# Attention output of a sliding-window layer: two PSUM halves copied out by ScalarE for both heads and added by GpSimd, in place of one ScalarE copy and two VectorE adds

## The chip, the core and the metric

The kernel runs on one core of a Trainium2 chip. A core has five engines, each with its own instruction stream that it works through in order: TensorE (PE in the profile, with PEld for its weight loads), VectorE (DVE), ScalarE (ACT), GpSimd (POOL) and SyncE (SP, which here only starts transfers). They share a large memory, SBUF, of 128 partitions. Matrix products land in PSUM, which has eight banks of 128 partitions by 512 float32 columns; GpSimd does not read PSUM in this kernel. The metric is the time in microseconds of one execution on the device, the median of several runs.

## What is computed

One layer of the reference, cut to what matters here (2048 tokens, width 2048, 32 query heads of 64, 4 key/value heads, blocks of 128 queries that see themselves and the 128 tokens before):

```python
q, k, v, gate = split(rms_norm(x) @ w_in)
q, k = rms_norm(q) * q_gain, rms_norm(k) * k_gain
s = einsum('bqhgd,bkhd->bhgqk', qj, kb) * scale + bias      # 128 queries against 256 keys
s = where(valid, s, -inf)
m = maximum(max(s), sink)
p = exp(s - m)
p = p / (sum(p) + exp(sink - m))
o = einsum('bhgqk,bkhd->bqhgd', p, vb)
return x + (o * silu(gate)) @ w_out
```

## The kernel before

The queries, keys and values are made by matrix products of 128 by 512 (`gemm`, lines 148, 151 and 154). To keep precision each float32 operand is split into a high part and a low remainder, and three products are added: high by high, high by low, low by high. One step of the plan `steps` makes 128 columns of the projection for 1024 tokens: 96 such products into two banks. There are two halves of the tokens (`c`), and in each two groups of one key step, one value step and eight query steps. While a step's products run, the attention of queries made earlier is put beside them (`beside`, which calls `unit`). After that come the gate's and the output's products, in a scheme with 7 instead of 8 quarter products; they fill the second half of the time, and the change does not touch them.

One call of `unit` handles two heads and two blocks of 128 queries; there are 128 calls. In order:

- `s` (two PSUM banks, one buffer): eight products of queries by keys, line 329. VectorE masks (line 337) and writes the biased scores into `lg` (line 342, four instructions), after which the two banks are free for the next unit.
- VectorE takes the row maximum, ScalarE four exponentials (line 355), VectorE the sum and its reciprocal, GpSimd the normalising product (line 360).
- `pt` (one bank, one buffer): four transposes on TensorE, line 364. ScalarE copies them as the high part `ph` (line 366), VectorE makes the remainder `pl` (line 368). Both have one buffer.
- GpSimd splits each by a triangle into the part of the earlier and of the current block: `php`, `plp` (line 372), `ph`, `pl` (line 374, in place), one buffer each.
- `o` (one bank, one buffer): up to eight products of values by probabilities, line 383. The values' tile `vv` holds the high parts in its first 64 columns and the remainders in the other 64, so partitions 0 to 63 of `o` hold the high half's result and partitions 64 to 127 the low half's. They have to be added. The two heads lie side by side in `o`'s columns; they are to end up below each other in `og`, one head in partitions 0 to 63 and the other in 64 to 127.
- Lines 385 to 390 do that, and are what the change edits.

```python
bot = at.tile([DH, 4, P], F32, tag="bot", name="bot", bufs=1)
nc.scalar.copy(out=bot, in_=o[DH:P])
og = at.tile([P, 2, P], F32, tag="og", name="og", bufs=1)
for h in range(2):
    nc.vector.tensor_tensor(out=og[h * DH:(h + 1) * DH], in0=o[0:DH, h::2, :], in1=bot[:, h::2, :], op=ALU.add)
```

The order of instructions on each engine is not the order of the code. The program is built with `schedule_with_timeline_sim=True`: a scheduler goes over all of it with its own estimates of durations, follows what each buffer and each operand permits, and writes out one fixed order for every engine. An edit in `unit` can thus move any instruction of the attention's stretch, on every engine. At run time an engine takes its instructions in that fixed order, and waits by semaphores.

Of the kernel before, what the change touches and what calls it, by code (L numbers as in the profile page):

```python
# [9 lines left out]
F32 = mybir.dt.float32  # L10
# [3 lines left out]
ALU = mybir.AluOpType  # L14
AX = mybir.AxisListType

P = 128
# [7 lines left out]
DH = 64  # L25
# [6 lines left out]
def swa_layer_kernel(ctx: ExitStack, tc: tile.TileContext, xT: bass.AP, x: bass.AP, w_in: bass.AP,  # L32
# [13 lines left out]
    nc = tc.nc  # L46
# [8 lines left out]
    at = attention.enter_context(tc.tile_pool(name="at", bufs=2))  # L55
# [263 lines left out]
    def unit(cb, j, qq, rq, kk, vv, bt):  # L319

        i0 = j % 4
        hs = slice(2 * cb, 2 * cb + 2)
# [30 lines left out]
        for b in range(2):  # L353
            for h in range(2):
# [6 lines left out]
                                op=ALU.mult)  # L361
# [16 lines left out]
        o = ps_o.tile([P, 4, P], F32, tag="o", name="o")  # L378
        for b in range(2):
            terms = [] if first and b == 0 else [(vv[:, i0 + b, :], p) for p in prev]  # L380
            terms += [(vv[:, i0 + b + 1, :], p) for p in cur]
            for i, (v, p) in enumerate(terms):
                nc.tensor.matmul(o[:, 2 * b:2 * b + 2, :], v, p[:, 2 * b:2 * b + 2, :],  # L383
                                 start=(i == 0), stop=(i == len(terms) - 1))
        bot = at.tile([DH, 4, P], F32, tag="bot", name="bot", bufs=1)
        nc.scalar.copy(out=bot, in_=o[DH:P])
        og = at.tile([P, 2, P], F32, tag="og", name="og", bufs=1)
        for h in range(2):
            nc.vector.tensor_tensor(out=og[h * DH:(h + 1) * DH], in0=o[0:DH, h::2, :], in1=bot[:, h::2, :], op=ALU.add)
        nc.sync.dma_start(out=o_sp[cb][:, j * P:(j + 2) * P], in_=og.rearrange("p b q -> p (b q)"))  # L390


# [29 lines left out]
    def beside(n):  # L422

        for cb, j in units.get(n, []):
            c, half = j // NB, j % NB // 4
            if (cb, c) not in bias:
                bias[cb, c] = load_bias(cb)
            if (cb // 4, c, half) not in kv:
                kv[cb // 4, c, half] = load_kv(cb // 4, c, half)
            qs, rq = queries[cb, c]  # L430
            unit(cb, j, qs[half], rq, *kv[cb // 4, c, half], bias[cb, c])
# [257 lines left out]
    for m, (p, i) in enumerate(tiles):  # L689
        kind, name = flat[p]  # L690
# [85 lines left out]
```

## Time and profile before

| what | value |
|---|---|
| median of 3 runs | 2465.68 us (2463.45 to 2465.91) |
| profiled execution, its own time | 2466.36 us |
| its span, first to last instruction | 2464.6 us |
| TensorE busy | 2431.2 us (99%) |
| VectorE, ScalarE, GpSimd busy | 1648.4, 971.6, 1092.3 us |
| stretch with attention | about 125 to 1303 us of the span |

The span is the time between the first and the last instruction in the trace; 1.8 us of the execution lie around it. Busy time of TensorE is a union of modelled intervals: products overlap, so a product of 512 columns shows 0.39 us and is followed by the next after 0.23. Idle time that an engine shows before an instruction is put down to whatever ended the wait.

### The profile page before, as it was taken

The page shows a single profiled execution, that of the slowest core. Times are in us where ns is not written, and L with a number is a line of the kernel's source. Part 1 is how long each engine was busy: PE and PEld are TensorE (multiplying, and loading weights), DVE is VectorE, ACT ScalarE, POOL GpSimd, SP SyncE. Part 2 cuts the span into 40 slices and gives each one's busy share as a digit, 9 for nine tenths or more (in the row PEclk, how much of TensorE's full clock was granted, in tenths as well). Part 3 has the DMA queues.
Part 4 walks back from the last instruction along what each step waited for, and adds up shares of the span by engine and source line. Part 5 has one row for each costly group of instructions (what it writes and reads, how often), then busy time and mean ns, then how long its engine had stood idle before and what let it go on. Part 6 is the DMA issues. An engine that isn't in the chain of part 4 may idle for free.

```text
span 2464.6 us, 35291 instructions
## 1 busy us (share of the span) xinstructions
PE 2431.2 (99%) x11858; PEld 2044.4 (83%) x11858; DVE 1648.4 (67%) x3206; ACT 971.6 (39%) x2387; POOL 1092.3 (44%) x1041
## 2 busy tenths in 40 slices
PE   8999999999999999999999999999999999999999
PEld 7888888887788888888887888888888888888887
DVE  7287777789777877887864776576684436554533
ACT  7255545456545545554543332222232212122110
POOL 0156666575656666666541343034451033113434
PEclk9999999999999999999999999999999999999999
DMA  7322333125331223212127997687887679678755
GB/s 228 104 95 90 109 98 119 59 68 172 107 105 57 78 63 105 86 52 84 65 86 269 316 363 257 236 271 260 263 271 260 224 228 346 213 265 278 262 181 175
DMA packets 211380, 429.39 MB, mean 174 GB/s; under 512 B 20208, under 2 KB 91520, under 8 KB 211200
## 3 DMA queue, kind: packets, MB, share of 16 engines
q1 hardware_dynamic: 211200, 427.15, 53.1%
q8 instruction: 94, 1.54, 0.3%
q14 instruction: 86, 0.70, 0.1%
HBM read 336.88 MB, written 90.19 MB: 173 GB/s over the span
## 4 chain that ended last, share of the span: by engine, by line
PE 87%; DMA 7%; DVE 3%; POOL 1%; issue 1%; ACT 1%; SPq 0%; DVEq 0%; POOLq 0%; ACTq 0%
PE acc L148 25%; PE acc L151 25%; PE acc L154 25%; PE s L329 5%; PE o L383 5%; DMA braw<-xT 2%; PE pt L364 2%; DMA out<-craw 1%; DMA craw<-x 1%; DMA raw<-xT 1%; DVE parts L520 0%; DMA braw<-t_sp 0%; POOL craw L523 0%; DVE braw L520 0%; DVE braw L572 0%
## 5 line engine op out<-in xcount | busy, mean ns | idle before, releaser
L148 PE MATMUL acc<-bigh,wh 128*128 128x512 f32 x1472 | 494.4, 396 | 7.7 <-ACT bigh L101 5.5
L154 PE MATMUL acc<-bigh,wl 128*128 128x512 f32 x1472 | 491.1, 394 | 0.0
L151 PE MATMUL acc<-bigl,wh 128*128 128x512 f32 x1472 | 490.5, 395 | 0.1
L523 POOL TENSOR_TENSOR craw<-craw,u 128x512 f32<-128x512 f32 x112 | 163.0, 1469 | 419.7 <-DMA craw<-x 229.1
L148 PEld LDWEIGHTS acc<-bigh,wh 128*128 128x128 f32 x1472 | 274.3, 190 | 58.3 <-ACT bigh L101 5.5
L151 PEld LDWEIGHTS acc<-bigl,wh 128*128 128x128 f32 x1472 | 275.2, 190 | 51.9 <-DVE bigl L102 1.3
L154 PEld LDWEIGHTS acc<-bigh,wl 128*128 128x128 f32 x1472 | 274.5, 190 | 50.5
L355 ACT ACTIVATE lg<-lg,nm 128x128 f32<-128x128 f32 x512 | 199.9, 392 | 185.0 <-DVE nm L348 169.2
L151 PE MATMUL acc<-obl,parts 128*128 128x512 f32 x768 | 236.6, 389 | 1.4 <-DVE obl L520 1.4
L154 PE MATMUL acc<-obh,parts 128*128 128x512 f32 x768 | 236.6, 389 | 0.4 <-DVE parts L520 0.4
L154 PE MATMUL acc<-obh,wl 128*128 128x512 f32 x768 | 236.5, 389 | 0.0
L148 PE MATMUL acc<-obh,parts 128*128 128x512 f32 x768 | 236.4, 389 | 0.0
L148 PE MATMUL acc<-obh,wh 128*128 128x512 f32 x768 | 236.4, 389 | 0.0
L151 PE MATMUL acc<-obl,wh 128*128 128x512 f32 x768 | 236.4, 389 | 0.0
L134 POOL TENSOR_TENSOR wl<-raw,wh 128x512 fp32r<-128x512 f32 x144 | 187.5, 1303 | 94.7 <-ACT wh L133 87.9
L523 POOL TENSOR_TENSOR araw<-araw 128x1024 f32<-128x1024 f32 x48 | 119.6, 2492 | 225.5 <-DMA araw<-o_sp 75.3
L360 POOL TENSOR_TENSOR lg<-lg,den 128x512 f32<-128x512 f32 x128 | 134.1, 1048 | 112.1 <-DVE den L359 74.0
L563 ACT CAST obh<-braw 128x1024 fp32r<-128x1024 f32 x80 | 83.9, 1053 | 230.1 <-DVE braw L520 108.7
L151 PEld LDWEIGHTS acc<-obl,parts 128*128 128x128 f32 x768 | 143.9, 188 | 31.8 <-DVE obl L520 2.2
L154 PEld LDWEIGHTS acc<-obh,parts 128*128 128x128 f32 x768 | 144.2, 188 | 30.9 <-DVE parts L520 0.9
L151 PEld LDWEIGHTS acc<-obl,wh 128*128 128x128 f32 x768 | 144.2, 188 | 30.0
L148 PEld LDWEIGHTS acc<-obh,parts 128*128 128x128 f32 x768 | 144.1, 188 | 30.1
(136 smaller groups left out, 4405.8 us busy)
## 6 DMA issues: line engine op xcount, KB each, us to landing
braw<-w_out SPq DMA_DIRECT2D x88, 512.0 KB, 5.6
araw<-w_in SPq DMA_DIRECT2D x80, 512.0 KB, 5.7
araw<-o_sp SPq DMA_DIRECT2D x80, 512.0 KB, 5.7
raw<-w_in SPq DMA_DIRECT2D x79, 512.0 KB, 3.7
braw<-xT SPq DMA_DIRECT2D x72, 512.0 KB, 5.8
craw<-o_sp SPq DMA_DIRECT2D x80, 256.0 KB, 4.9
o_sp<-og SPq DMA_DIRECT2D x128, 128.0 KB, 1.9
o_sp<-craw SPq DMA_DIRECT2D x64, 256.0 KB, 5.0
```

Of the source, the lines that this page charges most:

```text
L134: eng.tensor_tensor(out=l[:, a:b], in0=r, in1=h[:, a:b].bitcast(F32), op=ALU.subtract)
L148: nc.tensor.matmul(acc[n], h[:, cs], res[0][k][:, n * CH:(n + 1) * CH], start=(k == 0), stop=False)
L151: nc.tensor.matmul(acc[n], h[:, cs], res[1][k][:, n * CH:(n + 1) * CH], start=False, stop=False)
L154: nc.tensor.matmul(acc[n], l[:, cs], res[0][k][:, n * CH:(n + 1) * CH], start=False, stop=(k == last))
L329: nc.tensor.matmul(s[:, b, h, lo:], qq[:, h, (i0 + b) * P:(i0 + b + 1) * P], kk[:, i, (i0 + b) * P + lo:(i0 + b + 2) * P], start=(i == 0), ...
L355: nc.scalar.activation(out=lg[:, b, h], in_=lg[:, b, h], func=AF.Exp, bias=nm[:, b, h:h + 1], accum_out=den[:, b, h:h + 1])
L360: nc.gpsimd.tensor_tensor(out=lf, in0=lf, in1=den.rearrange("p b h -> p (b h)").unsqueeze(2).broadcast_to([P, 4, P]), op=ALU.mult)
L364: nc.tensor.transpose(out=t[:, i, :], in_=lf[:, i, :], identity=ident)
L383: nc.tensor.matmul(o[:, 2 * b:2 * b + 2, :], v, p[:, 2 * b:2 * b + 2, :], start=(i == 0), stop=(i == len(terms) - 1))
L523: nc.gpsimd.tensor_tensor(out=out, in0=a, in1=b, op=op)
L563: nc.scalar.copy(out=h, in_=src)
```

## The change

The row layout of `og` is made by the copies: for each head ScalarE copies its high half into `og`'s rows and its low half into the same rows of a new tile `ol`. GpSimd then adds the two whole tiles. `bot` goes; `og` and `ol` have two buffers each, where `bot` and `og` had one. Per unit one ScalarE instruction becomes four of half its columns, two VectorE instructions go, and one GpSimd instruction of 128 by 256 comes. The transfer that follows is as it was.

```diff
-        bot = at.tile([DH, 4, P], F32, tag="bot", name="bot", bufs=1)
-        nc.scalar.copy(out=bot, in_=o[DH:P])
-        og = at.tile([P, 2, P], F32, tag="og", name="og", bufs=1)
+        og = at.tile([P, 2, P], F32, tag="og", name="og")
+        ol = at.tile([P, 2, P], F32, tag="ol", name="ol")
         for h in range(2):
-            nc.vector.tensor_tensor(out=og[h * DH:(h + 1) * DH], in0=o[0:DH, h::2, :], in1=bot[:, h::2, :], op=ALU.add)
+            hs = slice(h * DH, (h + 1) * DH)
+            nc.scalar.copy(out=og[hs], in_=o[0:DH, h::2, :])
+            nc.scalar.copy(out=ol[hs], in_=o[DH:P, h::2, :])
+        nc.gpsimd.tensor_tensor(out=og, in0=og, in1=ol, op=ALU.add)
         nc.sync.dma_start(out=o_sp[cb][:, j * P:(j + 2) * P], in_=og.rearrange("p b q -> p (b q)"))
```

The scheduler's order moves with it. Three places follow. The names are those of the list above; `acc` is a projection's product, `s` the scores, `pt` the transposes, `o` the attention's result, and the four `o` rows of a block name the four probability tiles in turn.

TensorE at the end of the attention, where the projection's products of the last query step run out. Before:

```order
L151 MATMUL acc<-bigl,wh 128x512 x2
L154 MATMUL acc<-bigh,wl 128x512 x2
L364 MATMUL pt<-ident,lg 128x128 x4
L383 MATMUL o<-php,vv 128x256
L383 MATMUL o<-plp,vv 128x256
L383 MATMUL o<-ph,vv 128x256
L383 MATMUL o<-pl,vv 128x256
L383 MATMUL o<-php,vv 128x256
L383 MATMUL o<-plp,vv 128x256
L383 MATMUL o<-ph,vv 128x256
L383 MATMUL o<-pl,vv 128x256
L383 MATMUL o<-php,vv 128x256
```

After:

```order
L154 MATMUL acc<-bigh,wl 128x512
L383 MATMUL o<-php,vv 128x256
L364 MATMUL pt<-ident,lg 128x128 x4
L383 MATMUL o<-plp,vv 128x256
L383 MATMUL o<-ph,vv 128x256
L383 MATMUL o<-pl,vv 128x256
L383 MATMUL o<-php,vv 128x256
L383 MATMUL o<-plp,vv 128x256
L383 MATMUL o<-ph,vv 128x256
L383 MATMUL o<-pl,vv 128x256
L383 MATMUL o<-php,vv 128x256
L364 MATMUL pt<-ident,lg 128x128 x4
```

Before, the last transposes and one unit's `o` products stand behind the last projection products, and the next `o` row is the last unit's. After, one more unit's `o` products stand behind the last projection product, so that the last three units follow each other there.

TensorE around units 79 to 81 (counted from 0), in the middle of the second half of the tokens. Before:

```order
L364 MATMUL pt<-ident,lg 128x128 x4
L154 MATMUL acc<-bigh,wl 128x512
L148 MATMUL acc<-bigh,wh 128x512 x2
L383 MATMUL o<-php,vv 128x256
L151 MATMUL acc<-bigl,wh 128x512 x2
L383 MATMUL o<-plp,vv 128x256
L383 MATMUL o<-ph,vv 128x256
L154 MATMUL acc<-bigh,wl 128x512 x2
L148 MATMUL acc<-bigh,wh 128x512 x2
L151 MATMUL acc<-bigl,wh 128x512 x2
L383 MATMUL o<-pl,vv 128x256
L383 MATMUL o<-php,vv 128x256
```

After:

```order
L383 MATMUL o<-pl,vv 128x256
L329 MATMUL s<-kk,qq 128x256 x8
L383 MATMUL o<-php,vv 128x256
L364 MATMUL pt<-ident,lg 128x128 x4
L383 MATMUL o<-plp,vv 128x256
L383 MATMUL o<-ph,vv 128x256
L329 MATMUL s<-kk,qq 128x256 x8
L383 MATMUL o<-pl,vv 128x256
L383 MATMUL o<-php,vv 128x256
L383 MATMUL o<-plp,vv 128x256
L383 MATMUL o<-ph,vv 128x256
L383 MATMUL o<-pl,vv 128x256
```

Before, projection products stand between one `o` group and the next and inside them. After, the end of one unit's `o`, the scores of a later unit, the next unit's `o`, and the scores of the unit after that stand together with no projection product among them.

GpSimd at the same units. Before:

```order
L360 TENSOR_TENSOR lg<-lg,den 128x512
L134 TENSOR_TENSOR wl<-raw,wh 128x512
L372 AFFINE_SELECT php<-ph 128x512
L374 AFFINE_SELECT ph<-ph 128x512
L372 AFFINE_SELECT plp<-pl 128x512
L374 AFFINE_SELECT pl<-pl 128x512
```

After:

```order
L360 TENSOR_TENSOR lg<-lg,den 128x512
L372 AFFINE_SELECT php<-ph 128x512
L391 TENSOR_TENSOR og<-og,ol 128x256
L374 AFFINE_SELECT ph<-ph 128x512
L372 AFFINE_SELECT plp<-pl 128x512
```

The new add stands between the four selects of the next unit, here behind the first of them; in other units it stands behind the second or the third.

## Rows read from the trace of the kernel before

**Rows 1.** The page: span, busy us (share of the span) and instructions by engine.
```profile
span 2464.6 us, 35291 instructions
PE 2431.2 (99%) x11858; PEld 2044.4 (83%) x11858; DVE 1648.4 (67%) x3206; ACT 971.6 (39%) x2387; POOL 1092.3 (44%) x1041
```

**Rows 2.** Windows: stretch, its length, busy us (instructions) by engine, granted clock, DMA.
```profile
160.00:420.00 260.00, 251.60 (x1350) 215.55 (x1349) 197.73 (x523) 149.08 (x456) 165.79 (x187) 0.97 0.33 102
...
680.00:940.00 260.00, 260.00 (x1410) 223.82 (x1409) 201.61 (x514) 130.52 (x399) 163.53 (x186) 1.00 0.23 73
...
1200.00:1310.00 110.00, 106.14 (x571) 90.74 (x571) 75.27 (x189) 52.54 (x163) 49.98 (x69) 0.97 0.26 89
```

**Rows 3.** Waits of TensorE in the attention: total us, times, longest us.
```profile
PE s L329 <- DVE lg L342: 5.8, 5, 2.2
PE pt L364 <- DVE pl L368: 2.7, 3, 1.9
PE o L383 <- DVE og L389: 2.2, 1, 2.2
...
PE acc L148 <- DVE og L389: 1.3, 1, 1.3
PE s L329 <- DVE den L358: 1.0, 1, 1.0
```

**Rows 4.** Groups by shape: out<-in, shapes, count | busy us, mean ns | idle before.
```profile
L389 DVE TENSOR_TENSOR og<-o,bot 64x256 f32<-64x256 f32 x256 | 105.5, 412 | 11.2 <-ACT bot L386 9.2
...
L133 ACT CAST wh<-raw 128x512 fp32r<-128x512 f32 x151 | 93.1, 617 | 133.1 <-PE acc L151 127.3 <-POOL php L372 2.1 <-DMA raw<-w_in 1.6
...
L563 ACT CAST obh<-braw 128x1024 fp32r<-128x1024 f32 x80 | 83.9, 1053 | 230.1 <-DVE braw L520 108.7 <-DMA braw<-w_out 57.2 <-DVE braw L597 32.7
...
L386 ACT COPY bot<-o 64x512 f32<-64x512 f32 x128 | 74.8, 585 | 8.8 <-PE o L383 5.8
```

**Rows 5.** Line 523, GpSimd on SBUF operands: duration ns min/median/max.
```profile
L523 POOL TENSOR_TENSOR araw<-araw x48: 2385/2399/3166, 1478.0 to 2432.7; 128x1024 f32<-128x1024 f32 x48
L523 POOL TENSOR_TENSOR araw<-araw,craw x32: 1280/1294/2009, 1389.0 to 2070.6; 128x512 f32<-128x512 f32 x32
```

**Rows 6.** Timeline, TensorE, end of the attention: start us, us, instruction [idle before].
```profile
1295.99 0.28 PE L383 MATMUL o<-pl,vv 128*128 128x256 f32 x1
1298.51 0.35 PE L383 MATMUL o<-php,vv 128*128 128x256 f32 x1 [2.24 <-DVE og L389]
1299.02 0.39 PE L383 MATMUL o<-plp,vv 128*128 128x256 f32 x1 [0.15 <-POOL plp L372]
...
1299.72 0.58 PE L383 MATMUL o<-pl,vv 128*128 128x256 f32 x1 [0.20 <-POOL pl L374]
...
1302.84 0.76 PE L148 MATMUL acc<-bigh,wh 128*128 128x512 f32 x1 [1.26 <-DVE og L389]
```

**Rows 7.** Timeline, TensorE, between two steps, around 294 us.
```profile
294.50 1.16 PE L329 MATMUL s<-kk,qq 128*128 128x128 f32 x8 [1.69 <-DVE lg L342]
295.49 0.60 PE L364 MATMUL pt<-ident,lg 128*128 128x128 f32 x4
295.84 0.37 PE L383 MATMUL o<-php,vv 128*128 128x256 f32 x1
```

**Rows 8.** Timeline, TensorE, between two steps, around 224 us.
```profile
224.05 1.16 PE L329 MATMUL s<-kk,qq 128*128 128x128 f32 x8 [1.00 <-DVE den L358]
226.81 0.66 PE L364 MATMUL pt<-ident,lg 128*128 128x128 f32 x4 [1.60 <-POOL lg L360]
...
227.98 0.58 PE L383 MATMUL o<-plp,vv 128*128 128x256 f32 x1 [0.40 <-POOL plp L372]
```

**Rows 9.** Timeline, TensorE, one more such place, at 639 us.
```profile
639.54 1.16 PE L329 MATMUL s<-kk,qq 128*128 128x128 f32 x8 [2.16 <-DVE lg L342]
```

**Rows 10.** Windows over two of six spells of lower clock, columns as in the windows above.
```profile
296.10:299.50 3.40, 3.26 (x11) 2.73 (x11) 3.31 (x10) 2.33 (x10) 0.83 (x2) 0.50 0.61 187
...
1299.60:1306.40 6.80, 5.42 (x15) 4.17 (x16) 0.83 (x2) 1.66 (x3) 0.06 (x1) 0.50 0.38 114
```

## The prediction, made before the changed kernel ran

> **What bounds the kernel now.** I read the page first, for one question: which engine has no time left. TensorE is busy for 2431 of 2464.6 us [rows 1], so the kernel is as long as TensorE's work plus its waits, and work taken from another engine counts only where TensorE waits for it. The stretch with attention, about 125 to 1303 us, is the only one that the change touches. The windows show that TensorE waits there in two places: it is idle for 8.4 us in the stretch from 160 to 420 us and for 3.9 us at the attention's end, and not at all from 680 to 940 us, although VectorE has 202 of 260 us of work there [rows 2]. A busy VectorE alone is thus no cost here. Next come TensorE's own waits by cause: VectorE stands behind 13.0 us of them in all (5.8 + 2.7 + 2.2 + 1.3 + 1.0) [rows 3]. Third I looked where those waits lie, on the timeline. They are not spread out. They stand in bunches where the fixed order puts one unit's products right behind another's, with hardly a projection product between [rows 6 to 9]. That is what I then counted in the order after the change.
>
> **The work that moves.** VectorE loses 256 adds of 412 ns, 105.5 us [rows 4]. From 680 to 940 us there are 29 units, so its load falls from 202 to 178 of 260 us. None of that was on the path there.
>
> ScalarE loses 128 copies of 585 ns and gains 512 of half the columns. No row shows a copy of 64 by 256. The casts of 512 and 1024 columns take 617 and 1053 ns, 0.85 ns a column, and by that slope a copy of 256 takes 585 - 218 = 367 ns; the lower end is half of 585, 293 ns, the upper the 585 of the undivided copy [rows 4]. I take 0.37, nearest to the slope: four take 1.47 us, bounds 1.2 to 2.3. The time from `o`'s last product until its bank is free was one copy and two adds, 585 + 2 x 412 = 1.41 us. It stays what it was, 1.47, with bounds -0.2 to +0.9 us per unit. ScalarE's load from 680 to 940 us goes from 131 to 131 + 29 x (1.47 - 0.585) = 156 of 260 us: room enough.
>
> The Trainium skill, page "ScalarE: Activation LUTs", section "What ACT_TABLE_LOAD costs", gives 186 ns plus 0.833 ns per column, with neighbours overlapping by 93 ns. By an estimate from that page four copies take 4 x 399 - 3 x 93 = 1.3 us, and the forecast would be about 2 us lower, over 13 places; no row here shows the instruction.
>
> GpSimd gains 128 adds. With two full SBUF operands it takes 1294 ns for 512 columns and 2399 for 1024, 2.16 ns a column, so 256 take 0.74 us [rows 5]; bounds 0.65 (half of 1294) and 1.29. That is 95 us in all. Its load from 680 to 940 us goes from 164 to 185 of 260 us [rows 2]. On average nobody waits for it. But the add stands among the four selects of the next unit, and the last product of each block needs the last select: the way from a unit's transposes to the end of its `o` becomes 0.74 us longer wherever TensorE has nothing else to do. Where it has some 24 projection products in between (5.5 us at 0.23 us each), that is hidden.
>
> **The order, which carries the sum.** I counted in TensorE's order two kinds of crowding. First, units whose `o` begins with at most three projection products since the `o` before: 5 before (units 9, 17, 21, 53, 127, counted from 0), 18 after (8, 12, 16, 20, 39, 49, 52, 77, 80, 84, 111 to 114, 116, 125 to 127). Second, units whose scores begin with at most eight such products since the scores before: 5 before (12, 13, 20, 24, 56), 14 after (12, 16, 20, 24, 48, 56, 59, 80, 84, 87, 116, 118, 120, 126). Eleven of those 14 stand within an `o` pair of the first list; three (48, 59, 126) stand alone. The second list is a wait for `lg`, the first a wait for `o`'s bank and the selects, and both are set by buffers with one copy, whatever VectorE's load.
>
> The prices are read where the kernel before has such pairs. A bare pair, with nothing between: 2.24 + 0.15 + 0.20 = 2.6 us [rows 6]. A pair with scores and transposes between: 1.7 us in one place, where the wait for `lg` then covers `o`'s; 3.0 and 2.2 us in two others [rows 7 to 9]. I take 1.7, the place with the least other work queued, with 1.3 (the bare price less 1.3 us of scores and transposes) and 3.3 as bounds. Scores alone: 1.0 [rows 8].
>
> - Bare pairs: two more than before (125, 126), 2 x (2.6 + 0.74) = 6.7 us, and 0.7 for the add in the one that was there: 7.4.
> - The other eleven new pairs: 11 x 1.7 = 18.7 us (14 to 36).
> - Scores alone: three at 1.0, less one that goes: 2.0.
>
> That is 28 us.
>
> **The clock.** The granted clock was 0.50 of full in six spells of 3.4 or 6.8 us, all of which began within 3 us after a bunch of waits; two of them are shown [rows 10]. That is 1.2 in place of 2.4 GHz: a spell of 3.4 us gives up 1.7 us of work. Four of the five crowded places of before were followed by one. After, I count nine more crowded places (unit 12; 39; 49; 77; 80; 84; 111 to 114; 116; a longer end), 9 x 0.8 x 1.7 = 12 us. TensorE idles for part of a spell, 1.4 of 6.8 us in the last [rows 10], so I take 9, with 4 and 15 as ends.
>
> **Given back.** VectorE's waits do not all come from crowding; 2.7 us are waits for `pl` [rows 3], in the change of token halves, where VectorE is full. A lighter VectorE may save them: -3.
>
> **The sum.** The profiled execution took 2466.4 us, 0.7 above the median of the runs. 2466.4 + 28 + 9 - 3 = 2500 us, 1.4% slower. With the lower ends (7 + 14 + 2 + 4 - 5 = 22), of which half is left where waits overlap, it is 2478; with the upper 2466.4 + 9 + 36 + 3 + 15 = 2530.
>
> **The rivals.**
>
> *Faster: the lighter VectorE is what counts.* If the crowded products of the new order find their operands ready, because the units run earlier on a VectorE with 24 us more room in every 260, then TensorE's 13.0 us of waits for VectorE go, and most of the lower clock with them (two spells of 6.8 and four of 3.4 us, 27.2 us in all, 13.6 of work). All of it gives 2440 us, half of it 2453. This speaks for it: VectorE is the fullest engine after TensorE [rows 2]. Against it: the waits for the bank follow from one buffer and a chain of fixed lengths, and 1.41 us of that chain remain. It decides from the point where the new pairs cost under 0.5 us each. The Trainium skill names this way out: "Perfetto Trace Analysis", section "Optimizing Scalar/DVE Operations", says that handing work of a saturated VectorE to ScalarE or GpSimd may make sense, and adds that GpSimd shares a port with VectorE. Chance 0.09.
>
> *No change: the pairs are crowded on paper only.* The counted pairs cost what `s` and `pt` between them leave over, a few tenths each, 13 x 0.3 = 4 us, and the relief of 3 us meets it: 2467 us. Rows 7 speak for it, since there the second wait is nothing. Rows 6 and 8 speak against it. Chance 0.07.
>
> *Much slower: GpSimd becomes late for the projection.* It also makes the low parts of the weights (1.3 us each), in the same fixed order, and the new add waits for four ScalarE copies with those behind it. If a third of 32 steps started 1.3 to 2.6 us late on top, 14 to 28 us are added: 2514 to 2530 us and, with more of the lower clock, up to 2545. From 680 to 940 us GpSimd has 75 us left, which speaks against it. Chance 0.12.
>
> That the change does not do what it says is ruled out by the order: four copies and one add stand there.
>
> **How the numbers follow.** The forecast, slower by the crowding, has chance 0.72: 2500 us, its own range 2478 to 2530. About 0.2% (5 us) is what a measurement of this kernel can tell from no change. Faster by more: 0.09, the first rival. Within: 0.07 of the second rival and 0.01 of the forecast, 0.08. Slower: 0.71 + 0.12 = 0.83. The range of 2470 to 2530 leaves out the first two rivals (0.16) and a few per cent above, which the forecast's share below 2478 does not make up; 2468 takes in a part of the second.
>
> **What would show it.** In the changed kernel's windows TensorE is idle around 880 to 960 us (units 77 to 84) and from 1200 to 1260 (units 111 to 116), where it had hardly any idle time. Its waits name ScalarE's copies (`og`, `ol`) for `o`, where they named VectorE's add. The end of the attention has three bare pairs, each with 2 to 3.5 us of waits. VectorE's busy time falls by about 105 us, ScalarE's rises by about 113, GpSimd's by about 95. There are 10 to 16 spells of the lower clock. The prediction is wrong if the waits at the new pairs stay under half a microsecond, or if TensorE's waits there name the weights' `wl` in place of the units' tiles.

## The result, and the profile of the changed kernel

The changed kernel takes 2545.28 us (median of 5 runs, 2541.78 to 2546.24), the kernel before 2464.41 (2463.45 to 2465.91): ratio 1.0325, 95% interval 1.031 to 1.034. It is 81 us slower. The forecast was 2500 us, the range's upper end 2530.

The page's first lines, to be held against [rows 1] (span; busy us, share and instructions by engine):

```profile
span 2543.4 us, 35597 instructions
...
PE 2460.6 (97%) x11858; PEld 2059.4 (81%) x11858; DVE 1553.4 (61%) x2950; ACT 1073.4 (42%) x2771; POOL 1190.2 (47%) x1169
```

VectorE lost 95 us of work, ScalarE gained 102, GpSimd 98. The new operations, by shape, columns as in [rows 4]:

```profile
L390 ACT COPY ol<-o 64x256 f32<-64x256 f32 x256 | 94.6, 369 | 3.8
L389 ACT COPY og<-o 64x256 f32<-64x256 f32 x256 | 93.5, 365 | 5.3 <-issue 3.6 <-PE o L383 0.2
...
L391 POOL TENSOR_TENSOR og<-og,ol 128x256 f32<-128x256 f32 x128 | 94.7, 740 | 26.9 <-ACT ol L390 23.9 <-DVE part L220 0.8 <-DVE s L337 0.8
```

No engine but TensorE is near full, and the operations cost what they should. So the loss has to stand in TensorE: in its waits, or in products that take longer. Columns as in [rows 3]:

```profile
PE acc L148 <- ACT sq L217: 12.9, 12, 2.8
PE pt L364 <- DVE pl L368: 9.1, 7, 2.9
PE o L383 <- POOL plp L372: 6.9, 8, 1.5
PE acc L148 <- ACT bigh L101: 6.2, 3, 5.4
PE o L383 <- ACT ol L390: 6.1, 3, 2.4
PE s L329 <- DVE lg L342: 5.8, 9, 2.1
PE o L383 <- POOL ph L374: 5.3, 5, 1.2
PE o L383 <- POOL php L372: 5.1, 4, 2.4
PE o L383 <- POOL pl L374: 4.6, 8, 1.5
...
PE acc L154 <- DVE wl L134: 0.9, 2, 0.5
```

All rows of this view add up to 77.7 us in 78 waits, those of before to 28.6 in 27: 49 us more. The other 29 of the 79 us by which the span grew are busy time: the same 11,858 instructions took TensorE 2460.6 in place of 2431.2 us. The granted clock gives the larger part of that. TensorE was busy for 59 us at a granted clock of 0.50, in before for 25; at half rate that is 17 us more. The remaining 12 us were not taken apart; a product ahead of a wait shows its whole length, where otherwise the next one overlaps it, and there are 51 more waits.

The largest row was not foreseen: the first product into a bank of the projection waits for ScalarE's `sq` (line 217, in `evac_q`, which empties the banks of an earlier query step and frees them), 12.9 us in 12 places, where before had 1.0 us in one.

Windows, columns as in [rows 2]. In the first two before was never idle, and TensorE now is:

```profile
680.00:940.00 260.00, 256.47 (x1377) 219.27 (x1376) 163.48 (x428) 144.61 (x452) 174.92 (x198) 1.00 0.26 79
...
880.00:960.00 80.00, 75.37 (x410) 64.08 (x410) 57.81 (x153) 46.94 (x150) 54.65 (x66) 1.00 0.23 73
...
1200.00:1300.00 100.00, 90.50 (x470) 76.36 (x469) 68.67 (x184) 58.75 (x188) 59.64 (x77) 0.95 0.21 69
1364.00:1384.00 20.00, 12.05 (x38) 8.73 (x39) 4.71 (x13) 8.36 (x26) 10.52 (x16) 0.55 0.07 26
```

A growth at least as large as at the attention's end stands around the change of the token halves. Before, then changed:

```profile
420.00:680.00 260.00, 251.76 (x1336) 212.70 (x1335) 211.44 (x515) 139.44 (x394) 162.34 (x173) 0.99 0.33 102
420.00:680.00 260.00, 235.43 (x1200) 196.48 (x1200) 182.37 (x425) 150.19 (x437) 166.62 (x184) 0.96 0.27 88
```

TensorE is idle there for 24.6 us, in before for 8.2. 9.4 of the 12.9 us for `sq` lie in this window.

One crowded place, the second of the pieces of order shown ahead of the prediction, on TensorE's timeline (start us, us, instruction, idle before):

```profile
945.68 0.28 PE L383 MATMUL o<-pl,vv 128*128 128x256 f32 x1
946.44 1.19 PE L329 MATMUL s<-kk,qq 128*128 128x256 f32 x8 [0.48 <-DVE lg L342]
948.02 0.36 PE L383 MATMUL o<-php,vv 128*128 128x256 f32 x1 [0.40 <-issue]
948.22 0.60 PE L364 MATMUL pt<-ident,lg 128*128 128x128 f32 x4
949.97 0.39 PE L383 MATMUL o<-plp,vv 128*128 128x256 f32 x1 [1.15 <-POOL plp L372]
...
950.77 1.19 PE L329 MATMUL s<-kk,qq 128*128 128x256 f32 x8 [0.30 <-DVE den L358]
...
952.84 0.50 PE L148 MATMUL acc<-bigh,wh 128*128 128x512 f32 x1 [0.28 <-ACT sq L217]
```

Five waits in turn, 2.6 us, and the fifth is the projection's: the first product into the running step's second bank. None is long, and none names `o`'s bank. The next such place, at 981 to 989 us, has 0.66, 0.16, 2.94 and 0.95 us, 4.7 in all, the 2.94 for `pt` from `pl` and the 0.95 for `sq`.

### The profile page after: what moved, and what is told of

The parts are those of the page before. It is cut to its first block, busy times and chain, and to the rows that moved or that the text cites. A ratio compares the mean times of both kernels' runs of the same rounds, so it can differ in the third digit from the quotient of the medians.

```text
span 2543.4 us, 35597 instructions
## 1 busy us (share of the span) xinstructions
PE 2460.6 (97%) x11858; PEld 2059.4 (81%) x11858; DVE 1553.4 (61%) x2950; ACT 1073.4 (42%) x2771; POOL 1190.2 (47%) x1169
## 4 chain that ended last, share of the span: by engine, by line
PE 57%; DMA 2%; issue 2%; DVE 2%; ACT 1%; POOL 1%; SPq 0%; DVEq 0%; POOLq 0%; ACTq 0%
PE acc L148 18%; PE acc L151 18%; PE acc L154 18%; PE o L383 2%; PE s L329 2%; DMA braw<-xT 1%; PE pt L364 1%; DMA craw<-w_in 1%; DMA braw<-t_sp 0%; DVE lg L342 0%; POOL craw L525 0%; ACT lg L355 0%; DVE braw L574 0%; DMA o_sp<-craw 0%; ACT og L389 0%
## 5 line engine op out<-in xcount | busy, mean ns | idle before, releaser
L148 PE MATMUL acc<-bigh,wh 128*128 128x512 f32 x1472 | 515.0, 399 | 21.1 <-ACT sq L217 12.9
L151 PE MATMUL acc<-bigl,wh 128*128 128x512 f32 x1472 | 510.8, 398 | 1.8 <-DVE bigl L102 1.8
L154 PE MATMUL acc<-bigh,wl 128*128 128x512 f32 x1472 | 509.2, 397 | 0.9 <-DVE wl L134 0.9
L148 PEld LDWEIGHTS acc<-bigh,wh 128*128 128x128 f32 x1472 | 279.4, 191 | 78.0 <-ACT sq L217 16.2
L342 DVE SCALAR_TENSOR_TENSOR lg<-s,rq,bias 128x128 f32<-128x128 f32 x512 | 144.2, 343 | 90.6 <-PE pt L364 78.0
L372 POOL TENSOR_SCALAR_AFFINE_SELECT php<-ph 128x512 fp32r<-128x512 f32 x128 | 83.3, 651 | 199.6 <-ACT ph L366 199.5
L618 ACT CAST parts<-araw 128x512 fp32r<-128x512 f32 x96 | 59.5, 621 | 260.6 <-PE acc L154 100.1
L154 PEld LDWEIGHTS acc<-obh,parts 128*128 128x128 f32 x768 | 144.2, 188 | 30.4 <-DVE parts L522 0.5
```

Of the source, the lines that this page charges most:

```text
L148: nc.tensor.matmul(acc[n], h[:, cs], res[0][k][:, n * CH:(n + 1) * CH], start=(k == 0), stop=False)
L151: nc.tensor.matmul(acc[n], h[:, cs], res[1][k][:, n * CH:(n + 1) * CH], start=False, stop=False)
L154: nc.tensor.matmul(acc[n], l[:, cs], res[0][k][:, n * CH:(n + 1) * CH], start=False, stop=(k == last))
L342: nc.vector.scalar_tensor_tensor(out=lg[:, b, h], in0=s[:, b, h, P:], scalar=r, in1=bt[:, h, :], op0=ALU.mult, op1=ALU.add)
L372: nc.gpsimd.affine_select(out=dst, in_=src.bitcast(F32), pattern=[[0, 4], [-1, P]], compare_op=ALU.is_gt, fill=zero, base=0, channel_multi ...
L618: nc.scalar.copy(out=h, in_=r)
```

## The experiments

Counts "n and m pairs" are those of the prediction: n units whose `o` begins at most three projection products after the `o` before, and m units whose scores begin at most eight such products after the scores before. **Theory A:** GpSimd's added work makes the scheduler write an order with more crowded pairs, and the order is what costs. **Theory B:** the four copies and the add cost as they run, in the chain of each unit; the order is a side effect. Ratios are to the kernel before, run on the same chip (median 2462.84 for e1 to e4, 2463.92 for e5 to e8, 2464.08 for e9 to e12).

**e1: the add back on VectorE.** The changed kernel, with

```diff
-        nc.gpsimd.tensor_tensor(out=og, in0=og, in1=ol, op=ALU.add)
+        nc.vector.tensor_tensor(out=og, in0=og, in1=ol, op=ALU.add)
```

> The changed kernel, but its one add of 128 by 256 is done by VectorE instead of GpSimd; the four ScalarE copies stay. In TensorE's order it has 4 crowded o pairs and 3 crowded score pairs (before: 5 and 5, changed kernel: 18 and 14, counted as in the prediction). Theory A, GpSimd's added work makes the scheduler write a crowded order, and the order is what costs: about as before, 2455 to 2470 us. Theory B, the four copies in the chain from one unit's o to the next cost at run time: still 2500 us or more.

Measured: 2463.73 us, ratio 1.0002 (0.9992 to 1.0012), 4 and 3 pairs. With the add on VectorE the four copies cost nothing, in the order that the scheduler then writes.

**e2: an unneeded GpSimd add.** The kernel before, with one more instruction in each unit, whose result nobody reads:

```diff
+        ol = at.tile([P, 2, P], F32, tag="ol", name="ol", bufs=1)
+        nc.gpsimd.tensor_tensor(out=ol, in0=og, in1=og, op=ALU.add)
```

> The kernel before, with one GpSimd add of 128 by 256 per unit put on top, of og with itself into a tile that nobody reads; the path of the output is as before. 14 crowded o pairs and 14 score pairs. Theory A: nearly all of the loss appears though nothing waits for the added instruction, 2510 to 2550 us. Theory B: 2464 to 2475 us.

Measured: 2541.39 us, ratio 1.0315 (1.0299 to 1.0331), 14 and 14 pairs. Durations of that instruction (ns, shortest, median and longest), and then three of TensorE's longest waits:

```profile
L391 POOL TENSOR_TENSOR ol<-og x128: 603/612/1702, 156.2 to 1378.4; 128x256 f32<-128x256 f32 x128
```

```profile
PE o L383 <- POOL pl L374: 10.8, 15, 1.3
PE s L329 <- DVE lg L342: 8.3, 12, 1.8
PE pt L364 <- DVE pl L368: 6.8, 6, 2.4
```

128 instructions of 0.61 us on an engine that is less than half busy cost 79 us, nearly all of the change's loss. The copies and the longer way of the result are not needed for it. `og` has one buffer, which the new add holds while it reads; but the trace puts none of the waits of VectorE's next adds into `og` down to GpSimd.

**e3: two unneeded ScalarE copies.** The kernel before, with

```diff
+        ol = at.tile([P, 2, P], F32, tag="ol", name="ol", bufs=1)
+        for h in range(2):
+            nc.scalar.copy(out=ol[h * DH:(h + 1) * DH], in_=o[0:DH, h::2, :])
```

> The kernel before, with two ScalarE copies of 64 by 256 per unit from o into a tile that nobody reads; GpSimd has no added work. 8 crowded o pairs and 8 score pairs. Theory A: 6 pairs more than before at the 3.7 us that each of the changed kernel's 22 cost, 2475 to 2495 us. Theory B: two of the four copies' load and a later release of o's bank, 2480 to 2510 us.

Measured: 2496.38 us, ratio 1.0136 (1.0116 to 1.0157), 8 and 8 pairs: in B's range, 1 us above A's. It does not decide between them.

**e4: less of other work on GpSimd.** The changed kernel, with half of the weights' low parts (line 134) made by VectorE.

```diff
-        nxt = load_stat(stat_src(steps[n + 1]), eng=nc.gpsimd) if n + 1 < len(steps) else None
+        nxt = [part for q in range(2) for part in load_stat(stat_src(steps[n + 1]), [q], eng=(nc.vector, nc.gpsimd)[q])] \
+            if n + 1 < len(steps) else None
```

> The changed kernel, with half of the weights' low parts (line 134) made by VectorE instead of GpSimd, 1.3 us each; the new copies and the add stay. 13 crowded o pairs and 9 score pairs, 12 more than before. Theory A: GpSimd is as light as before the change, and the loss falls with the pairs to 2490 to 2515 us. Theory B: no gain, 2540 to 2550 us.

Measured: 2511.75 us, ratio 1.0193 (1.0176 to 1.021), 13 and 9 pairs. It is 49 us slower than before on the same chip, so 32 of the 81 us come back, within A's range.

So far A held, but for e3. In these runs more pairs and more time go together, so e5 to e8 were to show whether it is the pairs that count.

**e5 and e6: both kernels ordered in another way.** In each one word:

```diff
-    with tile.TileContext(nc, schedule_with_timeline_sim=True) as tc:
+    with tile.TileContext(nc, schedule_with_timeline_sim=False) as tc:
```

> The kernel before, its code unchanged, but the scheduler is told to use another of its two ways of ordering (without the simulated timeline), so that every engine gets another fixed order. It has 13 crowded pairs of o and 2 of scores, where before has 5 and 5. It serves as the partner of e6, the changed kernel ordered in that same way. Theory A (the order is what costs, at some 4 us for each further pair): about 2464 + 4 x 5 = 2484 us, between 2470 and 2520. Theory B (the order costs little; the four copies and the GpSimd add cost at run time): 2464 to 2470 us.

> The changed kernel (ScalarE's four copies, GpSimd's add) ordered in the other way, as e5. It has no crowded pair of o and 3 of scores. Theory A: the edit itself costs nothing; it is no slower than e5, 2450 to 2475 us, and if the pairs are what costs, faster than e5. Theory B: the edit costs some 80 us whatever the order: e5 plus 60 to 90 us.

Measured: 2810.52 us (ratio 1.1408, 1.1389 to 1.1427) for before's code, 2846.85 (1.1551, 1.1529 to 1.1573) for the changed: 36 us or 1.3% slower, though it has 0 and 3 pairs against 13 and 2. A's numbers miss by far, and so do B's (e5 near before, e6 60 us or more above e5). The count of pairs says nothing about an order of another kind. Here the edit cost 36 us without any added pair; whether by its work or by yet another order these two runs do not part. TensorE's waits say where, e5 and then e6:

```profile
PE pt L364 <- POOL lg L360: 33.2, 83, 1.6
...
PE o L383 <- POOL php L372: 11.4, 27, 0.9
```

```profile
PE pt L364 <- POOL lg L360: 44.0, 69, 5.2
PE o L383 <- POOL php L372: 35.7, 64, 1.4
```

Many small waits for the selects on GpSimd: 24 us more on the select `php` alone.

**e7 and e8: all the weights' low parts on VectorE**, once in e1 and once in before (`eng=nc.gpsimd` becomes `eng=nc.vector` in the line shown for e4).

> The copies as changed, the add by VectorE as in e1, and the low parts of all weights (line 134) made by VectorE in place of GpSimd. The order has 1 crowded pair of o and 2 of scores. GpSimd loses about 32 x 1.3 us for each quarter of the plan, VectorE gains it. Theory A: the few pairs that are left cost little, so it is the fastest of all, 2440 to 2462 us. A rival to A (the count of pairs is a stand-in for something else, VectorE's room above all): VectorE has no room left in the attention, 2465 to 2500 us.

> The kernel before with only the low parts of all weights (line 134) moved from GpSimd to VectorE: GpSimd has less to do and VectorE more, the attention's code is untouched. The order has 3 crowded pairs of o and 3 of scores. Theory A: 2450 to 2465 us. Its rival (room on VectorE decides, not the order): 2470 to 2500 us.

Measured: 2462.53 us (0.9996, 0.9983 to 1.0008) and 2463.53 us (1.0002, 0.9992 to 1.0013), with 1 and 2 and with 3 and 3 pairs. VectorE is at 69% of the span in e8, and the kernel loses nothing by it, so the rival of e7 and e8 falls. Fewer pairs than before has do not gain anything either: e7 was to be the fastest of all. No version beat the kernel before.

**e9 to e12: the order held fixed.** To part order and work, TensorE's 11,850 products were pinned in a given order, by edges that ask for issue order and not for completion; the scheduler still places the other engines' instructions. A kernel pinned to its own order gives the same program, instruction by instruction, so that pinning itself adds nothing.

```diff
         swa_layer_kernel(tc, *args, out)
+        pin(tc)
...
+    for a, b in zip(order, order[1:]):
+        tc.add_manual_dep(pe[b], pe[a].name, mybir.DependencyInfo(mybir.DependencyClass.NoSync, mybir.DependencyReason.DATA), reason="pin")
```

`pe` holds the products as the code makes them, `order` a table of their places in the other kernel's order.

> The changed kernel (four copies by ScalarE, the add by GpSimd), with TensorE's order pinned: edges that ask for issue order alone put all 11,850 of its products in the order of the kernel before; the scheduler places the other engines' work around that. 5 and 5 crowded pairs. Theory A (the order that the scheduler writes is what costs): 2455 to 2475 us. Theory B (the added GpSimd work and the copies cost at run time, the order is a stand-in for them): 2530 to 2550 us. Between the two (2480 to 2520): both.

> The other corner: the kernel before, its work untouched (one copy, two VectorE adds, no GpSimd add), with TensorE's products pinned to the order of the changed kernel. 18 and 14 crowded pairs. Theory A: 2520 to 2550 us, though GpSimd has no added work. Theory B: 2464 to 2475 us. Between the two: the crowded order needs the longer chain to cost its full price.

> e2 (before plus an unneeded GpSimd add of 128 by 256 for each unit) with TensorE's products pinned to the order of the kernel before. The add's 0.73 us stays on GpSimd 128 times. Theory A: 2460 to 2475 us, against the 2541 of e2. Theory B: 2530 to 2545 us.

> The changed kernel with TensorE's products pinned to the order of e7, the least crowded one (1 and 2 pairs). Theory A: as e9 or a little faster, 2450 to 2470 us, so that no fault is left in the change itself. Theory B: 2530 to 2550 us.

Measured, with the rest for comparison:

| kernel | TensorE's order | pairs | us | ratio, 95% interval |
|---|---|---|---|---|
| before | own | 5, 5 | 2464 | 1 |
| e10: before's work | of the changed | 18, 14 | 2573.54 | 1.0447, 1.0431 to 1.0463 |
| e9: the changed work | of before | 5, 5 | 2487.81 | 1.0092, 1.0075 to 1.0108 |
| changed | own | 18, 14 | 2545.28 | 1.0325, 1.031 to 1.034 |
| e11: e2's work | of before | 5, 5 | 2479.83 | 1.007, 1.0055 to 1.0085 |
| e2 | own | 14, 14 | 2541.39 | 1.0315, 1.0299 to 1.0331 |
| e12: the changed work | of e7 | 1, 2 | 2488.69 | 1.0101, 1.0086 to 1.0116 |

Neither theory takes all: e9 fell where both were expected, e10 above A's range, e11 and e12 5 and 19 us above theirs. In before's order the changed work costs 24 us, and the rest of the 81, 57 us, is TensorE's order. e2 and e11 split alike: 16 and 63. The other way round the new order costs before's work 109 us, and the changed work is 28 us faster in it. So the two parts have no one size, but the order is the larger on both ways. The new order is the slower one for either work, also for the one that it was written for: the changed kernel would have lost less than a third as much in the order of before. The scheduler, which goes by its own estimates, did not find that.

What costs 24 us in e9 can be seen (line numbers are 74 higher there, so that L457 is line 383, L448 line 374, L308 line 234). TensorE's waits, which in before were 0.4, 5.8 and 2.0 us for the same three:

```profile
PE o L457 <- POOL pl L448: 13.9, 10, 3.2
PE s L403 <- DVE lg L416: 8.3, 7, 2.2
...
PE o L457 <- POOL plp L446: 4.5, 7, 1.1
```

The last product of `o` waits for the last select. GpSimd's timeline before one of these, and TensorE's product behind it:

```profile
1074.91 0.64 POOL L446 TENSOR_SCALAR_AFFINE_SELECT php<-ph 128x512 fp32r<-128x512 f32 x1 [3.07 <-ACT ph L440]
1076.33 0.74 POOL L465 TENSOR_TENSOR og<-og,ol 128x256 f32<-128x256 f32 x1 [0.79 <-ACT ol L464]
1077.03 1.29 POOL L208 TENSOR_TENSOR wl<-raw,wh 128x512 fp32r<-128x512 f32 x1
1078.28 0.63 POOL L448 TENSOR_SCALAR_AFFINE_SELECT ph<-ph 128x512 fp32r<-128x512 f32 x1
1078.87 0.63 POOL L446 TENSOR_SCALAR_AFFINE_SELECT plp<-pl 128x512 fp32r<-128x512 f32 x1
1081.92 2.91 POOL L308 TENSOR_TENSOR rq<-aq,mhalf 128x16 f32<-128x16 f32 x1 [2.43 <-DVE den L433]
1084.80 0.63 POOL L448 TENSOR_SCALAR_AFFINE_SELECT pl<-pl 128x512 fp32r<-128x512 f32 x1
...
1085.48 0.58 PE L457 MATMUL o<-pl,vv 128*128 128x256 f32 x1 [2.33 <-POOL pl L448]
```

Between the four selects of one unit stand the new add, a weight's low part and a query step's `rq` (2.91 us, which itself waits 2.43 for VectorE). The last select starts 9.9 us after the first. Outside the crowded places there are six such waits for `pl`, 12.5 us in all. In five of them (238, 625, 1027, 1085 and 1121 us; 11.1 us) `rq` stands directly ahead of the last select, in the sixth (381 us) `rstd`, another use of GpSimd's power function (1.66 us). GpSimd's order around that is again the scheduler's: `rq` stands among a unit's selects 3 times in before, 8 times in e9 and 10 times in the changed kernel, and neither before nor the changed kernel waits for `pl` in any of these units. Before's TensorE order leaves too little room for such a late select in five of the eight units of e9; the new order leaves enough in all ten. e11, where only GpSimd's add is new, has 6.7 us in the first of these rows; its 16 us are two thirds of e9's 24.

In e10 (line numbers 89 higher) the waits for VectorE stand out, against the changed kernel's own in the section on the result:

```profile
PE s L418 <- DVE lg L431: 20.3, 18, 2.8
PE acc L237 <- ACT sq L306: 11.7, 7, 3.4
PE pt L453 <- DVE pl L457: 8.3, 5, 2.9
```

20.3 us for `lg`, where the changed kernel has 5.8 in that order: there the lighter VectorE seems to help, though the other engines' orders differ as well. And 11.7 us for `sq` without any added copy: that wait belongs to the order.

## Why the prediction was right in direction and short in size

**Durations and loads: right.** 0.37 us a copy forecast, 0.365 and 0.369 measured; 0.74 us for the add, 0.740 measured. VectorE -95 (forecast -105), ScalarE +102 (113), GpSimd +98 (95).

**Where: right as far as it went.** TensorE is idle at 880 to 960 us (4.6 us) and from 1200 to 1300 (9.5 us), and the attention's end is longer. Its three bare pairs wait 1.72, 2.41 and 1.96 us for `ol`, as forecast near the 2.24 of [rows 6]. But the prediction found before idle in two places only and passed over 420 to 680 us (8.2 us), where the changed kernel is idle for 24.6.

**The sum, term by term.** Two steps failed: the price of the order (37 us forecast, 57 measured) and what the work costs away from the crowded places (3 us of relief forecast, 24 us of cost measured). A crowded place is here all that stands between two projection products around one or more pairs: 5 places before, 18 after. Measured is the growth of TensorE's time, after less before.

| term | forecast, us | measured, us |
|---|---|---|
| the bare pairs at the end | 7.4 | 5.6 |
| waits inside the other crowded places (18.7 and 2.0) | 20.7 | 28.2 |
| wait of the projection product behind a place | none | 5.6 |
| waits elsewhere | -3 | 10 |
| lower clock | 9 | 17 |
| other growth of TensorE's busy time | none | 12 |
| sum | 34 | 79 |

**The order: the first step that failed, by its size.** With bare pairs, scores and clock it came to 28 + 9 = 37 us. In its own work the order costs 57 (after less e9). The pair's price of 1.7 us was read at one place of before [rows 7], where the only wait is for `lg`; the four such places of before took 1.3 to 3.5 us. The eleven places of the changed kernel where an `o` pair meets a score pair took 1.6 to 3.8, on average 2.7. TensorE waits there for more than `lg` and `o`'s bank: in all 18 places 17.5 us for GpSimd's four selects and 9.0 for `pl`, which frees `pt`'s one bank, where the five of before have 1.0 and nothing. The 9.0 is nearly all of the row `pt` from `pl`, in which the sum put 3 us of relief.

The order also shows why the next projection product waits. Of the 32 pairs (18 and 14) 30 stand where that product is the first into a bank: 22 at a second bank (17 of them behind 36 products of the first bank of a projection step, 5 in the gate's first products) and 8 where a step or a gate's product begins. The banks of a query step are emptied by `evac_q`, on ScalarE and VectorE. The row `acc` from `sq` has no term in the sum: 5.6 of its 12.9 us stand directly behind crowded places, the other 7.3 in five waits at places that the count of pairs does not hold. In the changed kernel 20 of the 37 projection steps behind the first three have 20 or more products of the first bank ahead of the second bank's first, in before 11. Why the second bank's products could not stand earlier in the order was not tried.

**The clock: low, by the same cause.** Forecast 9 us (4 to 15), measured 17: with more waits there are more spells. Within the span there are eleven spells of the lower clock, before had six (forecast 10 to 16); the longest, at the attention's end, shows in the windows above as a mean of 0.55 over 20 us.

**What was costed at nothing outside the pairs: the second step that failed.** The prediction held that TensorE's waits stand in bunches at the pairs, and that the add is hidden wherever some 24 projection products lie between a unit's transposes and its `o`. Of before's 20 us of waits in the attention 9 already stood elsewhere. And e9 puts a price on the work: 24 us in before's order, where the sum had 3 of relief; TensorE waits there for the last select up to 3.2 us at a time. The error is in taking the add's 0.74 us as the delay. On an engine that works in order the last select is late by all that now stands ahead of it, here by `rq`'s 2.9 us too.

**The rivals.** The faster one is refuted as a whole. Its mechanism may be at work in the new order, where the changed work is 28 us faster than before's (e10 against after), net of what GpSimd's add costs there; that it is VectorE's relief was not shown alone, and it is less than what the order costs. The paper pairs are refuted by the 18 places: each of them waits, 0.6 us at the least. The much slower one, GpSimd late for the weights, came out at the right time for the wrong reason: its 2514 to 2545 us reach up to the result, yet TensorE waits for `wl` 0.9 us in all. GpSimd was late, as it said, but for the units' selects.

**The Trainium skill.** "Perfetto Trace Analysis", section "Optimizing Scalar/DVE Operations", says that handing work of a saturated VectorE to ScalarE or even GpSimd may make sense, and doubts that it helps between VectorE and GpSimd. VectorE stood at 67% of the span, so the page's condition is not met here, and no run tests the shared port that it gives as the reason. That the move did not help agrees with its doubt: e2 and e11 show a loss by GpSimd's work alone, and e1, with the same copies and VectorE adding, loses nothing.

**What stays open.** The two parts are measured with TensorE's order alone held fixed. 11 of e9's 24 us stand behind `rq`; what they would be with GpSimd's order held fixed too, and the add's duration alone new, was not run. The second buffers of `og` and `ol` are part of the changed work in every run and were not parted from it. Why the scheduler writes the new order is not shown, only that GpSimd's added work is enough for one of its kind (e2). And pairs below five gain nothing (e7, e8), while e12, with 1 and 2 pairs, is no faster than e9: the count is a sign of units that are late, not the cost itself.

## What to carry to other kernels

Where a scheduler fixes the order of in-order engines, an added instruction is charged with what it displaces: compare the orders first, and look at every wait of a crowded place, and at what stands behind it (here the second bank of the running step), before pricing it. Price what lies outside such places too. An engine that is less than half busy can still hold what the fullest one waits for; before moving work to it, look at what queues behind (here four short selects). To part the work from the order, pin one kernel's work to the other's order, both ways round; it takes two runs, and the four corners show whether the parts add up. They also show whether the scheduler's own order is the better one; here it was not.

## What the runs showed of the hardware

ScalarE's copy of 64 by 256 from PSUM takes the same 0.35 to 0.37 us (512 copies of the changed kernel, medians 0.365 and 0.369) whether it writes to the partitions it reads or to the other half. GpSimd's add of 128 by 256 took 0.74 us with two different tiles (changed kernel) and 0.61 us with one tile read twice (e2). Its power function on 128 by 16 (`rq`) takes 2.9 us, four times the add of sixteen times as many elements: in the attention the longest instruction in GpSimd's queue is one of the smallest.
